# Hybrid decoder trunk with a product-key expert FFN: expert-slot transposes later among the hidden rows, the second half's first hidden rows in other PSUM banks, score products right behind the norms

## The chip, the cores and the metric

The kernel runs on one core of a Trainium2 chip. The metric is the device time of one execution in microseconds (us). The engines named below are PE (matrix products and transposes, into PSUM), DVE (vector work), ACT (activation functions and copies), POOL (elementwise work) and SP, which issues the transfers. Each engine works through its own list of instructions in the order in which the built program has them; an instruction that waits holds up everything behind it in that list.

## What is computed

Two layers; each adds an attention mixer and then an expert FFN to the residual `h`. The change lies in the expert FFN, which is in short:

```python
q = (xt @ wq).reshape(t, 8, 2, 128)
s = einsum('thpd,hpnd->thpn', q, sub_keys)        # scores: 8 heads x 2 halves x 64 keys per token
s_top, i_top = top_k(s, 16)
cand_s = s_top[:, :, 0, :, None] + s_top[:, :, 1, None, :]
best_s, best_j = top_k(cand_s, 16)                # 16 of 4096 experts per head and token
g = softmax(best_s)
h_all = xt @ u.T                                  # every token against all 4096 experts
a = gelu(h_all at the chosen experts) * g
out = (a scattered into t x 4096) @ v
```

## The kernel before

The 1040 tokens are four quarters. In each layer the FFN handles two halves of the tokens, P (quarters 0 and 1) and Q (quarters 2 and 3), one after the other; each half has two parts, called half 0 and half 1 in the code. The work of one such pair runs through these steps:

- `scores` (L987): PE products of the tokens with the keys; ACT copies the results out of PSUM (L992).
- `tops` (L996 to L1000): DVE takes the 16 best of 64 scores, five instructions for one group of 64 (`top16`). `combine` (L1018 to L1096) sums pairs, takes the best 16 of 64 candidates with `top16` again, makes the softmax (its result, `gS`, is written at L1045) and decodes the expert numbers into `mS` (L1092) and `rS` (L1094). All of it is DVE work but an exponential on ACT.
- `slots` (L1131, L1132, L1136): for each tile of 128 tokens PE transposes `mS`, `rS` and `gS` through PSUM banks 0 and 1 (ring `g`). DVE copies the first two out (L1133, L1134); ACT and DVE (L1139, L1140) read the third.
- `hidden` (L1113): for each of 32 rows of 128 experts PE forms `xt @ u.T` in 24 products of 512 columns (or 48 of 272 and 256), from weights that are split into a high and a low part. ACT applies gelu and writes row r of `G`.
- `gates` (DVE L1152 to L1157, PE L1164, DVE L1169): for 16 tokens at a time the choices are turned into a mask with 32 products and multiplied into `G`. In both calls that have gates they run among the later hidden rows, and need the slots.
- `values` (L1203): 32 rows of `G` times `v`, for 4 of the 8 output blocks (`d0`=0), then for the other 4 (`d0`=4). ACT and DVE split each row of `G` into high and low (L1196, L1197). At the end DVE adds the sums to `h` (L261, in `hupdate`), which frees the PSUM banks 4, 5, 6, 7, 2, 3 that held them.

While PE works on P's values, the choices for Q are prepared: `select` is a generator of norms (`apply`), then tops and combines of Q, and `values` takes steps of it after each row as long as a budget lasts (`bud`); what is left over is emitted by `run(todo)` before `hidden(l, Q, ...)`.

A scheduler then fixes the order on each engine, by a simulation of its own, under the dependences that the code order gives: an instruction that reuses a PSUM bank or a buffer stands behind the earlier users of it in the code. So the order on PE and DVE differs from the order in the code, and is read from the built program.

Of the kernel before, what the change touches and what calls it, by code (L numbers as in the profile page):

```python
# [22 lines left out]
LAG = 1  # L23
HQ = 8
PR = 13
START = 0
MM = ((3, 0, 2, 0, 0, 3, 0, 0), (3, 0, 2, 0, 0, 3, 0, 0))
PEND = 31
# [31 lines left out]
def tile_trunk(ctx, tc, h0, w_pk, wgate, w2, glab, w_out, wqT, keysT, u_pk, v_w, sinks,  # L60
# [100 lines left out]
    def set_rings(**kw):  # L161
        for tag, bs in kw.items():
            rings[tag] = [bs, 0]

    def ps1(tag="a"):
        r = rings[tag]
        r[1] += 1
        return banks[r[0][(r[1] - 1) % len(r[0])]]

    set_rings(d=(0, 1), o=(2,), a=(3, 4, 5, 6, 7), h=(6, 7, 2, 3), g=(0, 1), s=(4, 5), v=(4, 5, 6, 7, 2, 3))  # L170


    ident = const.tile([128, 128], F32, name="ident")
# [828 lines left out]
    def tops(P, half, cc):  # L1002

        nt = len(P.parts[half][1].tiles)
        V = sb([128, 3, 8, 16], F32, "V")
        I = sb([128, 3, 8, 16], U32, "I")
        P.V[half, cc] = V, I
        for a in range(8):
            for j in range(nt):
                top16(sv(P, half, 2 * cc + a // 4)[:, j, a % 4, :], V[:, j, a], I[:, j, a])  # L1010
                yield 1.3
# [84 lines left out]
    def cuts(P, halves):  # L1096

        if len(halves) == 2 and P.merge:
            return [(None, 0, P.sp.w)]
        return [(h, P.parts[h][0], P.parts[h][1].w) for h in halves]  # L1100

    def hidden(l, P, G, lo, hi, ring, cst=None, end=32):

        cs = cuts(P, (0, 1))
        for r in range(lo, hi):
            pss = [ps1(ring)[:, 0:w] for h, o, w in cs]
            for k in range(KT):
                if k % 4 == 0:
                    wh, wl = wpiece(u_pk[l, r][:, k * 128:(k + 4) * 128], f"u{l}_{r}_{k // 4}")
                ks = slice(k % 4 * 128, k % 4 * 128 + 128)  # L1110
                for i, (wt, low) in enumerate(((wh, 0), (wh, 1), (wl, 0))):
                    for ps, (h, o, w) in zip(pss, cs):
                        PE.matmul(ps, wt[:, ks], yv(h, low, k, 0, w // 2 if h is None else w),  # L1113
                                  start=(k == 0 and i == 0), stop=(k == KT - 1 and i == 2))
            for ps, (h, o, w) in zip(pss, cs):
                n = min(max(sum(P.gated) - o, 0), w)
                if n:
                    ga = sb([128, 512], F32, "ht")
                    ACT.activation(ga[:, 0:n], ps[:, 0:n], AF.Gelu)
                    POOL.tensor_tensor(G[:, r, o:o + n], ga[:, 0:n], G[:, r, o:o + n], op=ALU.mult)  # L1120
                if n < w:
                    ACT.activation(G[:, r, o + n:o + w], ps[:, n:w], AF.Gelu)
            P.rows = r + 1
            while cst and sum(P.gated) < P.sp.w and sum(P.gated) * (end - lo) < P.sp.w * (r + 1 - lo):
                gates(P, int(P.gated[0] == P.parts[0][1].w), G, *cst)

    def slots(P, half):

        for j, (o, m) in enumerate(P.parts[half][1].tiles):
            tp = ps1("g").bitcast(F16)[:, 0:256].rearrange("p (a b) -> p a b", a=2)  # L1130
            PE.transpose(tp[:, 0, 0:m], P.mS[0:m, j, :], ident16[0:m, 0:m])  # L1131
            PE.transpose(tp[:, 1, 0:m], P.rS[0:m, j, :], ident16[0:m, 0:m])  # L1132
            DVE.tensor_copy(P.mT[half][:, o:o + m], tp[:, 0, 0:m])  # L1133
            DVE.tensor_copy(P.rT[half][:, o:o + m], tp[:, 1, 0:m])  # L1134
            tg = ps1("g")
            PE.transpose(tg[:, 0:m], P.gS[0:m, j, :], ident[0:m, 0:m])  # L1136
            g4 = tg[:, 0:m].rearrange("p (b t) -> p b t", t=4)
            gh, gl = [P.gg[half][:, o // 4:(o + m) // 4, a] for a in range(2)]
            ACT.activation(gh, g4, AF.Copy, scale=GSC)  # L1139
            DVE.scalar_tensor_tensor(gl, g4, GSC, gh, op0=ALU.mult, op1=ALU.subtract)  # L1140
# [33 lines left out]
    def values(l, P, G, halves, d0, todo=iter(()), work=(), bud=0.0, hs=None, reuse=True):  # L1174


        cs = cuts(P, halves)
        work = dict(work)
        accs = [[None] * len(cs) for d in range(4)]
        for i, (h, o, w) in enumerate(cs):  # L1180
            for d in range(4):
                if w <= 256 and d % 2:
                    accs[d][i] = (bank[:, 256:256 + w], False, True)
                else:
                    bank = ps1("v")
                    accs[d][i] = (bank[:, 0:w], True, w > 256)
        done = []
        left = 0.0
        for r in range(32):
            wh, wl = wpiece(v_w[l][:, r, d0 * 128:d0 * 128 + 512], f"v{l}_{r}_{d0}" if reuse else None)  # L1190
            parts = []
            for h, o, w in cs:
                tg = "2" if w > 272 else ""
                ah = sb([128, w], F32R, "ah" + tg)
                al = sb([128, w], F32R, "al" + tg)
                ACT.activation(ah, G[:, r, o:o + w], AF.Copy)  # L1196
                last = DVE.tensor_tensor(al, G[:, r, o:o + w], ah.bitcast(F32), op=ALU.subtract)  # L1197
                parts.append((ah, al))
            done.append(last.ins)
            for d in range(4):  # L1200
                for i, (wt, low) in enumerate(((wh, 0), (wh, 1), (wl, 0))):
                    for (ps, opens, closes), pr in zip(accs[d], parts):
                        PE.matmul(ps, wt[:, d * 128:d * 128 + 128], pr[low], start=(opens and r == 0 and i == 0),  # L1203
                                  stop=(closes and r == 31 and i == 2))
            if r in work:
                work.pop(r)()
            if len(done) > LAG:
                left += bud
                with tc.issue_after(done[-1 - LAG]):
                    while left > 0:  # L1210
                        left -= next(todo, 99)
        for d in range(4):
            for (ps, _, _), (h, o, w) in zip(accs[d], cs):
                for half in (0, 1) if h is None else (h,):
                    sp = P.parts[half][1]
                    p = ps[:, half * sp.w:half * sp.w + sp.w] if h is None else ps
                    if hs is not None and half == 1:
                        DVE.tensor_tensor(hs[:, d0 + d], hs[:, d0 + d], p, op=ALU.add)
                        continue
                    ht = hload(2 * l + 1, d0 + d, sp)  # L1220
                    hupdate(2 * l + 2, d0 + d, sp, ht, p)
        return todo

    def run(*gens):
        for _ in itertools.chain(*gens):
            pass
# [40 lines left out]
    for l in range(DEPTH):  # L1267
# [49 lines left out]
            run(combine(P, 0, 0, *tabs), combine(P, 0, 1, *tabs))  # L1317
        for c in range(4):
            scores(l, P, c, (1,), "s")
        slots(P, 0)  # L1320
        run(tops(P, 1, 0), combine(P, 1, 0, *tabs))
        hidden(l, P, G, 0, 4, "h")
        run(tops(P, 1, 1), combine(P, 1, 1, *tabs))
        slots(P, 1)
        rb = rstd(2 * l + 1, qs[2])
        rb2 = rstd(2 * l + 1, qs[3])
        hidden(l, P, G, 4, PR, "h")
        hidden(l, P, G, PR, 32, "h", cst, PEND)
        Q = peer_setup(qs[2], qs[3], False)
        scored = []  # L1330

        def select():

            for q, x, r in ((qs[2], Y[0], rb), (qs[3], Y[1], rb2)):
                for k in range(KT):
                    apply(2 * l + 1, q, gf, x, r, (k,), buf="xb")
                    yield 1.0
            for half in range(2):
                for cc in range(2):
                    for gen in (tops(Q, half, cc), combine(Q, half, cc, *tabs) if half == 0 else iter(())):  # L1340
                        while len(scored) < 2 * cc + 2:
                            yield 99
                        yield from gen
                if half == 0:
                    slots(Q, 0)

        work = {5 * c + 9: lambda c=c: scored.append(scores(l, Q, c, (0, 1), "g")) for c in range(4)}
        todo = values(l, P, G, (0, 1), 0, select(), work, 2.4)
        todo = values(l, P, G, (0, 1), 4, todo, (), 1.8)
        run(todo)  # L1350
        hidden(l, Q, G, 0, HQ, "h")
        run(combine(Q, 1, 0, *tabs), combine(Q, 1, 1, *tabs))
        slots(Q, 1)
        hidden(l, Q, G, HQ, 32, "h", cst, QE)
        more = l + 1 < DEPTH
        if more:
            rb = rstd(2 * l + 2, quarters[0])
# [86 lines left out]
```

## Time and profile before

| | |
|---|---|
| median of three runs | 3353.25 us (3343.89 to 3354.38) |
| the profiled execution | 3348.59 us, span of its instructions 3346.8 us |
| PE busy | 3139.3 us, 94% of the span |
| DVE busy | 2074.0 us, 62% |
| ACT, POOL busy | 1311.1 us (39%), 958.4 us (29%) |
| granted PE clock, mean | 0.959 |

The span runs from the first to the last instruction; 1.8 us of the execution lie around it. Busy shares are means over the whole program: the FFN has stretches in which DVE works without a pause while PE waits for it.

### The profile page before, as it was taken

To read this page: it belongs to the slowest core of one execution; us is meant where nothing else is said; L and a number is where in the kernel's file an instruction comes from. 1 tells how busy PE (TensorE), PEld (TensorE's weight loads), DVE (VectorE), ACT (ScalarE), POOL (GpSimd) and SP (SyncE) were. 2 spreads that over 40 slices of the span, in tenths; PEclk is the share of its full clock that TensorE was granted. 3 is DMA by queue.
4 is the path that set the end of the run, shared out by engine and by line. 5 is a ranking of instruction groups with operands and counts; after the bars stand their busy time and mean duration, and the time that the engine had idled before them with its cause. 6 is when DMAs were issued, how large, how long until landed. Compare 5 with 4: busy or idle time off the path is not lost.

```text
span 3346.8 us, 65733 instructions
## 1 busy us (share of the span) xinstructions
PE 3139.3 (94%) x23453; PEld 2636.6 (79%) x23453; DVE 2074.0 (62%) x6694; ACT 1311.1 (39%) x3013; POOL 958.4 (29%) x976
## 2 busy tenths in 40 slices
PE   7999999988999988999898999999889999899998
PEld 7686887768999987888874878877668888688788
DVE  4546446689885389753225464457796835986457
ACT  4534334424334343324344343344333344343354
POOL 4314021313454341010401131213244524301135
PEclk9899998989999999999997999999799999999999
DMA  8767774736346555446964677757454466554665
GB/s 292 235 194 251 248 258 136 215 127 236 128 137 191 182 174 172 157 145 200 333 232 141 211 263 241 251 161 238 149 181 148 154 191 219 172 179 143 195 191 169
DMA packets 406442, 655.56 MB, mean 196 GB/s; under 512 B 44560, under 2 KB 122464, under 8 KB 406112
## 3 DMA queue, kind: packets, MB, share of 16 engines
q1 hardware_dynamic: 406112, 651.35, 60.3%
q8 instruction: 184, 3.01, 0.4%
q14 instruction: 146, 1.20, 0.1%
HBM read 492.70 MB, written 158.47 MB: 195 GB/s over the span
## 4 chain that ended last, share of the span: by engine, by line
PE 67%; DVE 20%; DMA 7%; ACT 2%; issue 2%; SPq 1%; POOL 1%; DVEq 0%; POOLq 0%; ACTq 0%
PE b L1113 18%; PE b L1203 15%; PE b L335 13%; PE b L1164 4%; PE b L987 3%; PE b L703 2%; DVE arena_r L1197 2%; DMA arena<-h 2%; DVE arena L998 2%; DVE arena L1000 2%; DVE arena L997 2%; PE b L618 2%; PE b L757 2%; DMA arena<-in_w_pk_dram 1%; DVE arena L999 1%
## 5 line engine op out<-in xcount | busy, mean ns | idle before, releaser
L281 POOL TENSOR_TENSOR arena_r<-arena,arena_r 128x512 fp32r<-128x512 f32 (+1 forms) x440 | 555.4, 1268 | 869.5 <-ACT arena_r L274 800.3
L1113 PE MATMUL b<-arena_r 128*128 128x512 f32 (+2 forms) x3840 | 763.0, 357 | 17.5 <-DVE arena L261 15.5
L1203 PE MATMUL b<-arena_r 128*128 128x512 f32 (+2 forms) x4224 | 749.7, 337 | 31.4 <-DVE arena_r L1197 24.6
L1203 PEld LDWEIGHTS b<-arena_r 128*128 128x128 f32 x4224 | 643.8, 190 | 126.2 <-DVE arena_r L1197 35.7
L335 PE MATMUL b<-arena_r 128*128 128x256 f32 (+1 forms) x4992 | 702.6, 295 | 36.4 <-ACT arena_r L274 10.0
L1113 PEld LDWEIGHTS b<-arena_r 128*128 128x128 f32 x3840 | 626.0, 191 | 115.6 <-DVE arena L261 16.2
L335 PEld LDWEIGHTS b<-arena_r 128*128 128x128 f32 x4992 | 643.9, 196 | 76.3 <-issue 19.7
L274 ACT ACTIVATE arena_r<-arena 128x512 fp32r<-128x512 f32 x456 | 285.1, 629 | 479.8 <-PE b L1113 104.1
L1197 DVE TENSOR_TENSOR arena_r<-arena,arena_r 128x512 fp32r<-128x512 f32 (+2 forms) x352 | 270.8, 783 | 314.6 <-ACT arena_r L1196 313.5
L308 ACT ACTIVATE arena_r<-arena 128x512 fp32r<-128x512 f32 x288 | 181.2, 631 | 384.3 <-PE b L1203 120.9
L987 PE MATMUL b<-arena_r 128*128 128x256 f32 (+1 forms) x1632 | 208.9, 283 | 3.4 <-DMA arena_r<-m_3l 1.8
L987 PEld LDWEIGHTS b<-arena_r 128*128 128x128 f32 (+1 forms) x1632 | 196.5, 183 | 13.5 <-issue 4.4
L1152 DVE TENSOR_TENSOR arena<-arena 128x2048 f16<-128x2048 f16 x129 | 176.1, 1367 | 45.3 <-PE b L1164 45.3
L257 POOL TENSOR_TENSOR arena<-arena 128x256 f32<-128x256 f32 (+1 forms) x126 | 107.9, 856 | 315.1 <-ACT arena L256 312.4
L1120 POOL TENSOR_TENSOR arena<-arena 128x32 f32<-128x32 f32 (+25 forms) x91 | 98.5, 1089 | 305.4 <-ACT arena L1171 206.6
L1196 ACT ACTIVATE arena_r<-arena 128x512 fp32r<-128x512 f32 (+2 forms) x352 | 172.2, 502 | 31.1 <-PE b L1203 27.6
L1164 PEld LDWEIGHTS <-arena 128*128 128x128 f16 x4128 | 144.4, 118 | 17.2 <-issue 14.4
L1169 DVE SCALAR_TENSOR_TENSOR arena<-b,arena 128x224 f32<-128x224 f32 (+20 forms) x129 | 63.1, 499 | 145.9 <-PE b L1164 145.7
L1164 PE MATMUL b<-arena 128*128 128x32 f16 x4128 | 152.3, 190 | 0.0
L715 DVE TENSOR_TENSOR_SCAN arena<-arena,zf 128x384 f32<-128x384 f32 (+6 forms) x116 | 104.1, 900 | 76.5 <-ACT arena L710 75.5
L421 ACT ACTIVATE arena<-b 128x256 f32<-128x256 f32 (+1 forms) x144 | 55.2, 384 | 211.7 <-PE b L335 211.2
L1157 DVE TENSOR_TENSOR arena<-arena 128x1024 f16<-128x1024 f16 x129 | 123.3, 956 | 0.1
(267 smaller groups left out, 3796.7 us busy)
## 6 DMA issues: line engine op xcount, KB each, us to landing
arena<-in_v_w_dram SPq DMA_DIRECT2D x288, 256.0 KB, 2.9
arena<-in_u_pk_dram SPq DMA_DIRECT2D x256, 256.0 KB, 3.0
arena_r<-a_0h SPq DMA_DIRECT2D x108, 256.0 KB, 3.7
arena_r<-a_0l SPq DMA_DIRECT2D x108, 256.0 KB, 3.9
arena_r<-a_1h SPq DMA_DIRECT2D x108, 256.0 KB, 3.2
arena_r<-a_1l SPq DMA_DIRECT2D x108, 256.0 KB, 3.5
arena<-m SPq DMA_DIRECT2D x96, 256.0 KB, 4.5
arena<-h SPq DMA_DIRECT2D x192, 128.0 KB, 3.1
```

Source lines behind the costliest of these rows:

```text
L274: ACT.activation(hi, src, AF.Copy)
L281: e.tensor_tensor(lo[:, a:b], src[:, a:b], hi[:, a:b].bitcast(F32), op=ALU.subtract)
L308: ACT.activation(hi, wload(src), AF.Copy)
L335: PE.matmul(ps, wt[:, ks], x.at(low, k, xo, sp.w), start=(k == 0 and i == 0), stop=(k == KT - 1 and i == 2))
L987: PE.matmul(ps, yv(half, low, k, o, m), wt[:, kk * 256:kk * 256 + 256], start=(k == 0 and i == 0 and e == 0), stop=(k == KT - 1 and i == 2 ...
L1113: PE.matmul(ps, wt[:, ks], yv(h, low, k, 0, w // 2 if h is None else w), start=(k == 0 and i == 0), stop=(k == KT - 1 and i == 2))
L1152: DVE.tensor_tensor(Lh, iotaM.unsqueeze(1).to_broadcast([128, 4, 128, 4]), v4(P.mT[half], 128), op=ALU.is_equal)
L1157: DVE.tensor_tensor(R, R0.unsqueeze(2).to_broadcast([128, 4, 2, 32, 4]), P.gg[half][:, t0 // 4:t0 // 4 + 4].unsqueeze(3).to_broadcast([128 ...
L1164: PE.matmul(ps[:, i * 32:(i + 1) * 32], Lh[:, b, :, t], R[:, b, part, :, t], start=(part == 0), stop=(part == 1))
L1196: ACT.activation(ah, G[:, r, o:o + w], AF.Copy)
L1197: last = DVE.tensor_tensor(al, G[:, r, o:o + w], ah.bitcast(F32), op=ALU.subtract)
L1203: PE.matmul(ps, wt[:, d * 128:d * 128 + 128], pr[low], start=(opens and r == 0 and i == 0), stop=(closes and r == 31 and i == 2))
```

## The change

Three things are moved. In the first half, the transposes of P's half 0 come after six hidden rows where they came before the first, with the combines of half 1 behind them, and those of half 1 stand at hidden row 19 (`PR + 6`), among the gates, where they came before row 4. In the second half, the first eight hidden rows use the PSUM banks 0, 1, 6, 7 (ring `hq`) where they used 6, 7, 2, 3, and the transposes of Q's half 1 stand at row 16 where they came before row 8. During P's values, the four score products of Q stand behind rows 8, 10, 12, 14 where they stood behind rows 9, 14, 19, 24; each then adds 9.0 to the budget, and the budgets per row are 2.1 and 1.6 where they were 2.4 and 1.8, with 0.8 charged for a norm where it was 1.0.

```diff
+HS = 8
...
-    set_rings(d=(0, 1), o=(2,), a=(3, 4, 5, 6, 7), h=(6, 7, 2, 3), g=(0, 1), s=(4, 5), v=(4, 5, 6, 7, 2, 3))
+    set_rings(d=(0, 1), o=(2,), a=(3, 4, 5, 6, 7), h=(6, 7, 2, 3), hq=(0, 1, 6, 7), g=(0, 1), s=(4, 5), v=(4, 5, 6, 7, 2, 3))
...
-    def hidden(l, P, G, lo, hi, ring, cst=None, end=32):
+    def hidden(l, P, G, lo, hi, ring, cst=None, end=32, jobs=()):
 
         cs = cuts(P, (0, 1))
+        jobs = dict(jobs)
         for r in range(lo, hi):
+            if r in jobs:
+                jobs[r]()
...
             if r in work:
-                work.pop(r)()
+                left += work.pop(r)() or 0.0
...
+        run(tops(P, 1, 0))
+        hidden(l, P, G, 0, 6, "h")
         slots(P, 0)
-        run(tops(P, 1, 0), combine(P, 1, 0, *tabs))
-        hidden(l, P, G, 0, 4, "h")
-        run(tops(P, 1, 1), combine(P, 1, 1, *tabs))
-        slots(P, 1)
+        run(combine(P, 1, 0, *tabs), tops(P, 1, 1), combine(P, 1, 1, *tabs))
         rb = rstd(2 * l + 1, qs[2])
         rb2 = rstd(2 * l + 1, qs[3])
-        hidden(l, P, G, 4, PR, "h")
-        hidden(l, P, G, PR, 32, "h", cst, PEND)
+        hidden(l, P, G, 6, PR, "h")
+        hidden(l, P, G, PR, 32, "h", cst, PEND, {PR + 6: lambda: slots(P, 1)})
...
                     apply(2 * l + 1, q, gf, x, r, (k,), buf="xb")
-                    yield 1.0
+                    normed.append(k)
+                    yield 0.8
...
-        work = {5 * c + 9: lambda c=c: scored.append(scores(l, Q, c, (0, 1), "g")) for c in range(4)}
-        todo = values(l, P, G, (0, 1), 0, select(), work, 2.4)
-        todo = values(l, P, G, (0, 1), 4, todo, (), 1.8)
+        def score(c):
+            assert len(normed) == 2 * KT
+            scores(l, Q, c, (0, 1), "g")
+            scored.append(c)
+            return 9.0
+
+        work = {2 * c + HS: lambda c=c: score(c) for c in range(4)}
+        todo = values(l, P, G, (0, 1), 0, select(), work, 2.1)
+        todo = values(l, P, G, (0, 1), 4, todo, (), 1.6)
         run(todo)
-        hidden(l, Q, G, 0, HQ, "h")
+        hidden(l, Q, G, 0, HQ, "hq")
         run(combine(Q, 1, 0, *tabs), combine(Q, 1, 1, *tabs))
-        slots(Q, 1)
-        hidden(l, Q, G, HQ, 32, "h", cst, QE)
+        hidden(l, Q, G, HQ, 32, "h", cst, QE, {HQ + 8: lambda: slots(Q, 1)})
```

In the changed file the lines stand a few numbers lower: the hidden products L1113 are L1117 there, the transposes L1131, L1132 and L1136 are L1135, L1136 and L1140, the value products L1203 are L1207. (So an L1136 means `gS` in a row of before, and `rS` in a row of the changed program.)

What the scheduler makes of it is shown at two places. The first is PE's list where Q's hidden rows begin, in layer 0 (layer 1 has the same pattern). Names are the PSUM bank written (`b0_65` is bank 0) and the buffers read; `x12` is twelve such instructions in a row. Before:

```order
L1203 MATMUL b3_68<-arena_r_63 128x256 x5
L1113 MATMUL b2_67<-arena_r_63 128x512 x12
L1113 MATMUL b6_71<-arena_r_63 128x512 x24
L1113 MATMUL b7_72<-arena_r_63 128x512 x22
L1136 MATMUL b0_65<-ident_73,arena_64 128x128
L1113 MATMUL b7_72<-arena_r_63 128x512 x2
L1113 MATMUL b2_67<-arena_r_63 128x512 x12
L1113 MATMUL b3_68<-arena_r_63 128x512 x14
L1136 MATMUL b0_65<-ident_73,arena_64 128x128
L1113 MATMUL b3_68<-arena_r_63 128x512 x10
L1113 MATMUL b6_71<-arena_r_63 128x512 x24
L1113 MATMUL b7_72<-arena_r_63 128x512 x24
```

Behind these 144 products come the transposes L1131 of `mS` and L1132 of `rS`, apart from each other, with 8 and 27 products between them. After:

```order
L1207 MATMUL b3_68<-arena_r_63 128x256 x5
L1117 MATMUL b6_71<-arena_r_63 128x512 x12
L1140 MATMUL b0_65<-ident_73,arena_64 128x128 x2
L1117 MATMUL b0_65<-arena_r_63 128x512 x24
L1117 MATMUL b6_71<-arena_r_63 128x512 x12
L1117 MATMUL b7_72<-arena_r_63 128x512 x12
L1135 LDWEIGHTS arena_64
L1135 MATMUL b1_66<-ident16_78,arena_64 128x128
L1136 LDWEIGHTS arena_64
L1136 MATMUL b1_66<-ident16_78,arena_64 128x128
```

Both transposes of `gS` moved from behind 58 and 86 products to behind 12, and those of `mS` and `rS` from behind 144 to behind 60. Hidden row 0 now writes bank 0 and row 1 bank 1, which the transposes of `slots(Q, 0)`, earlier in the code, use too, so both stand behind them. After the rows shown a second L1135 and L1136 follow at once, then 24 products in bank 1; the first gate products (L1168) stand behind 216 hidden products, where they stood behind 277.

The second place is PE's list in the first half of layer 1, from the end of hidden row 4 on. Before:

```order
L1113 MATMUL b7_72<-arena_r_63 128x512 x2
L1131 LDWEIGHTS arena_64
L1131 MATMUL b1_66<-ident16_78,arena_64 128x128
L1113 MATMUL b7_72<-arena_r_63 128x512 x9
L1132 LDWEIGHTS arena_64
L1132 MATMUL b1_66<-ident16_78,arena_64 128x128
L1113 MATMUL b7_72<-arena_r_63 128x512 x13
L1113 MATMUL b2_67<-arena_r_63 128x512 x9
```

After:

```order
L1117 MATMUL b7_72<-arena_r_63 128x512 x24
L1135 LDWEIGHTS arena_64
L1135 MATMUL b1_66<-ident16_78,arena_64 128x128
L1136 LDWEIGHTS arena_64
L1136 MATMUL b1_66<-ident16_78,arena_64 128x128
L353 MATMUL b0_65<-ones_82,arena_64 128x1
L1117 MATMUL b2_67<-arena_r_63 128x512 x24
L1117 MATMUL b3_68<-arena_r_63 128x512 x5
```

The first transpose of `mS` moved from behind 122 hidden products to behind 144, that of `rS` from behind 131 to behind 144 as well. The six transposes of half 1, which before stood behind 218 to 288 products, stand behind 484 and 505 now, past the first gates.

## Rows read from the trace of the kernel before

**Rows 1.** Waits of PE over the whole span: us in total, times, longest.

```profile
PE b L1203 <- DVE arena_r L1197: 24.6, 27, 2.7
PE b L1131 <- DVE arena L1092: 17.2, 4, 7.5
PE b L1113 <- DVE arena L261: 15.5, 2, 9.6
...
PE b L1136 <- DVE arena L1045: 7.5, 3, 5.1
...
PE b L1136 <- DVE arena L1140: 4.1, 4, 1.6
```

**Rows 2.** Stretches: start:end, length, busy by engine (instructions), granted PE clock, DMA.

```profile
780.00:840.00 60.00, 47.99 (x388) 47.11 (x388) 60.00 (x331) 20.47 (x40) 29.41 (x20) 0.96 0.55 178
...
1176.00:1287.00 111.00, 101.34 (x760) 98.60 (x760) 101.03 (x501) 44.23 (x99) 39.58 (x32) 0.94 0.54 171
...
1296.20:1300.30 4.10, 4.06 (x11) 3.23 (x12) 4.10 (x33) 1.46 (x4) 1.57 (x3) 0.62 0.41 132
1300.30:1331.00 30.70, 30.70 (x135) 24.85 (x134) 30.70 (x187) 14.62 (x24) 2.88 (x3) 1.00 0.61 193
...
2923.00:2957.00 34.00, 34.00 (x140) 27.26 (x140) 34.00 (x211) 16.64 (x28) 3.60 (x4) 0.93 0.57 183
```

**Rows 3.** PE in order of time, layer 0, first half: start, length, [idle before].

```profile
839.69 0.19 PE L1131 MATMUL b<-ident,arena 16*128 16x16 f16 x1 [7.54 <-DVE arena L1092]
839.81 3.66 PE L1113 MATMUL b<-arena_r 128*128 128x256 f32 x15
```

**Rows 4.** PE in order of time, layer 1, first half.

```profile
2472.26 0.29 PE L1131 MATMUL b<-ident,arena 128*128 128x128 f16 x1 [6.35 <-DVE arena L1092]
2472.30 4.19 PE L1113 MATMUL b<-arena_r 128*128 128x512 f32 x9
...
2502.99 0.48 PE L1136 MATMUL b<-ident,arena 128*128 128x128 f32 x1 [5.14 <-DVE arena L1045]
...
2536.68 2.31 PE L1164 MATMUL b<-arena 128*128 128x32 f16 x64
```

**Rows 5.** DVE in order of time, layer 1, first half.

```profile
2482.20 0.21 DVE L1134 COPY arena<-b 128x128 f16<-128x128 f16 x1
...
2513.24 3.46 DVE L1152 TENSOR_TENSOR arena<-arena 128x2048 f16<-128x2048 f16 x2
...
2518.97 0.69 DVE L1157 TENSOR_TENSOR arena<-arena 128x1024 f16<-128x1024 f16 x1
```

**Rows 6.** PE in order of time, layer 0, where Q's hidden rows begin.

```profile
1283.83 2.75 PE L1203 MATMUL b<-arena_r 128*128 128x272 f32 x21
1296.24 15.13 PE L1113 MATMUL b<-arena_r 128*128 128x512 f32 x58 [9.65 <-DVE arena L261]
...
1317.83 13.68 PE L1113 MATMUL b<-arena_r 128*128 128x512 f32 x58
1331.35 0.23 PE L1131 MATMUL b<-ident,arena 128*128 128x128 f16 x1
```

**Rows 7.** DVE in order of time, in the same stretch.

```profile
1284.32 0.43 DVE L1197 TENSOR_TENSOR arena_r<-arena,arena_r 128x256 fp32r<-128x256 f32 x1
...
1308.31 0.28 DVE L1045 TENSOR_TENSOR arena<-arena 128x128 f32<-128x128 f32 x1
...
1329.53 0.43 DVE L1092 COPY arena<-arena 128x128 f16<-128x128 f16 x1
...
1331.43 0.43 DVE L1094 COPY arena<-arena 128x128 f16<-128x128 f16 x1
```

**Rows 8.** Layer 1, where Q's hidden rows begin: PE, then DVE.

```profile
2922.66 15.00 PE L1113 MATMUL b<-arena_r 128*128 128x512 f32 x54 [5.89 <-DVE arena L261]
...
2957.70 0.23 PE L1131 MATMUL b<-ident,arena 128*128 128x128 f16 x1
...
2954.51 0.43 DVE L1092 COPY arena<-arena 128x128 f16<-128x128 f16 x1
```

More of the change, by code (lines that the diff above doesn't have):

```diff
@@ L1319, in tile_trunk @@
             scores(l, P, c, (1,), "s")
+        run(tops(P, 1, 0))
+        hidden(l, P, G, 0, 6, "h")
         slots(P, 0)
-        run(tops(P, 1, 0), combine(P, 1, 0, *tabs))
-        hidden(l, P, G, 0, 4, "h")
-        run(tops(P, 1, 1), combine(P, 1, 1, *tabs))
-        slots(P, 1)
+        run(combine(P, 1, 0, *tabs), tops(P, 1, 1), combine(P, 1, 1, *tabs))
         rb = rstd(2 * l + 1, qs[2])
         rb2 = rstd(2 * l + 1, qs[3])
-        hidden(l, P, G, 4, PR, "h")
-        hidden(l, P, G, PR, 32, "h", cst, PEND)
+        hidden(l, P, G, 6, PR, "h")
+        hidden(l, P, G, PR, 32, "h", cst, PEND, {PR + 6: lambda: slots(P, 1)})
         Q = peer_setup(qs[2], qs[3], False)
-        scored = []
+        scored, normed = [], []
         def select():
```

## The prediction, on record before the changed kernel ran

> **What bounds the kernel now.** The page's busy times come first: PE works 94% of the span, DVE 62%. So the end is set by PE's own work and by the moments at which it waits. The waits of PE, summed by what they waited for, show where [rows 1]. Two kinds belong to this change: transposes of `slots` that wait for the choices on DVE (17.2 + 7.5 + 4.1 = 28.8 us in 11 waits) and the first hidden rows of the second half, which wait until DVE has emptied a PSUM bank of `values` (15.5 us in two waits, one per layer). Together 44.3 us, 1.3% of the span; that is the most that moving instructions past these waits could give, the half clock behind them aside. A third kind, 24.6 us in 27 waits, is `values` waiting for DVE's low parts.
>
> Then the stretches [rows 2]. While PE stands at slots or at a bank, DVE is not late by chance: it is busy 60.00 of 60.00 us in 780 to 840, 30.70 of 30.70 in 1300.3 to 1331, 34.00 of 34.00 in 2923 to 2957. In these stretches DVE sets the time at which choices are ready, and PE's list only decides how much other work PE has done by then. That is the question to ask of each move: **how many hidden products stand ahead of a transpose, and when does DVE deliver what it reads?** A transpose that moves back in the list lets PE do more first; one that moves forward makes PE wait longer, however few the other waits become.
>
> The prices: a hidden product of 512 columns takes 13.68/58 = 0.236 us at full clock [rows 6]; one DVE instruction in the busy stretches takes 101.03/501 = 0.20 us on average [rows 2].
>
> **First half, layer 0.** Before, PE stands 7.54 us at 839.69, at the first transpose of `mS`, with 367 hidden products done [rows 3]. DVE has no gap from 780 on, and up to the L1092 that ends this wait its order is the same in both programs but for one 0.3 us instruction. So this time stays. In the new order 360 products and two transposes of `gS` stand ahead of that point; the waits ahead of it grow together instead of going away (the second transpose of `gS` waits for DVE's copy of the first, which now stands close to that same L1092). No gain to here. Behind it the transposes of half 1 are gone from the path to the gates: [rows 1] less the three long waits of [rows 3, 4] (7.54, 6.35, 5.14) leave 9.8 us in eight short ones, of which I put 4 us here. The half clock behind 839.81 is paid in both. With about 2 us for fewer broken stretches and 1 to 2 us lost again at the transposes that now stand among the gates I take **-4 us**. Bounds: -8 (nothing lost there) and +1 (the one long wait costs more clock).
>
> **First half, layer 1.** Here the gain is real. At 2472.26 a wait of 6.35 us ends, behind 122 products, and the next nine products take 4.19 us where 2.1 would do [rows 4]. In the new order 144 products stand ahead, and `rS` follows at once; it is written some 3.5 us behind `mS`, so at about 2476.3 PE has done 144 where it had done 131: 3 us won. From there to the first gate products at 2536.68 before takes 60.4 us for 205 products, 48.4 us of work; the rest is the wait of 5.14 us at 2502.99, smaller ones and half clock. After, 192 products (45.3 us) and one wait: the second tile's transposes need bank 1, which DVE's copies free; these stand 38 instructions behind L1092 before, ending at 2482.4 [rows 5], and 57 behind it now, so about 4.5 us later, near 2487, while PE arrives near 2483. Gates could begin at 2476.3 + 45.3 + 4.5 = 2526. DVE has the first masks (L1152) done at 2516.7 and starts on what multiplies them at 2519.0 [rows 5], so it is ready. That is 10.5 us won; less 1.5 for the transposes among the gates, **-9 us**. Bounds -14 (no wait at the copies) and -4 (DVE as late as PE).
>
> **Second half, layer 0.** The bank wait before is 9.65 us, then 58 products take 15.13 us, 1.4 more than at full clock [rows 6]. Banks 0 and 1 are not held by `values`, but `slots(Q, 0)` uses them, and it stands ahead of the hidden rows in the code; so hidden row 0 is behind the transposes of `gS`, and row 1 behind those of `mS` and `rS`. In the new order PE has only 12 products, in bank 6, ahead of the first, and 60 ahead of the other pair. When does DVE deliver? Before, from its last L1197 at 1284.32 to L1045 at 1308.31, L1092 at 1329.53 and L1094 at 1331.43 [rows 7]; between the first and L1092 stand 218 instructions, and 233 in the new order: 15 x 0.20 = 3 us more. Ahead of that, between the same two L1197 that bound the second part of `values`, 321 stand where 353 stood: 32 x 0.20 = 6.4 us less, since 13 groups of `top16` now run ahead of it where 9 did. So 3.4 us earlier by work, and up to 10 us more if the gaps in 1176 to 1287 (111.00 - 101.03) all closed [rows 2]. I take 5 us: L1092 near 1325. L1094 and DVE's copies between the two pairs add some 4 us, so at 1329 PE has 60 products done. Before it has 144 at 1331.35, thus 134 at 1329. **74 products behind, 74 x 0.236 = +17.5 us.** Behind this point both lists hold the same work for PE, and before has no wait there to win back. Bounds: all gaps closed, L1092 at 1316, gives 60 products at 1320.5, where before has 98: +9. No gain from `values` and the 15 instructions in full: 60 at 1337 against 168: +25.5.
>
> The scores move ahead without a price on PE: the same products stand in another place, and before their results were used it was DVE that idled. The budgets give little: while the scores are missing the generator answers 99, so `left` falls near -97, and even four times 9.0 doesn't bring it above zero before this call of `values` ends, in either version. The 13 groups come from the part that `run(todo)` emits and the scheduler hoists.
>
> **Second half, layer 1.** The same order, and nearly the same trace: a bank wait of 5.89 us, DVE without a gap, L1092 at 2954.51 and 152 products done at 2957.70 [rows 8]. With 5 us as above PE has 60 at 2954 against 136: **+18 us**, bounds as above.
>
> **The clock.** Behind the bank wait the granted clock is 0.62 for 4.1 us, a mixture of the two levels of 1.2 and 2.4 GHz, and 1.00 after that [rows 2]: one wait of 9.65 us costs about 1.5 us more. The new order has several waits in a row in each second half; I add 1 us a layer, since most of the slow work falls into time in which PE would wait anyway. The Trainium skill ("TensorE: Matmul & The Clock Gate", "What's actually happening") puts it the other way about: throttled is the default, and activity releases it. By that rule each wait of the row could start again at the low level, and as an estimate from it the sum would be some 4 us higher; no row here shows several waits that close together.
>
> **Sum.** -4 - 9 + 17.5 + 18 + 2 = +24.5 us on the profiled execution's 3348.6 (1.8 us of it around the span): **3373 us**. That execution lies 4.7 us under the median of the three runs, 3353.25, and inside their spread of 10.5 us; 0.3% is 10 us, about what a measurement of this kernel can tell from no change.
>
> **Rivals.** *The waits really go (faster).* Were `gS` and `mS` of the second half ready when PE comes to them, the bank waits (9.65 + 5.89 and some 3 of half clock) would vanish on top of the first halves' 13: about 3317 to 3330. It decides at L1045 and L1092: they would have to come some 18 us earlier, near 1290 and 1311. For it speaks that DVE idles in the first part of `values`, so that work could go there; against it that only four more groups do, in the new order. Chance 0.10. *It evens out.* `values` loses its waits on DVE, all gaps close, and the second halves cost +9 each against -13 or -18: 3346 to 3358. For it speak the 24.6 us of waits in [rows 1]. Chance 0.17. *Worse.* No gain in `values`, each wait with its own slow stretch: +25 a layer, little won in the first halves: 3392 to 3405. Chance 0.10. *As forecast,* 3358 to 3392: 0.63.
>
> The range leaves out the tail on each side: 3348 to 3392. Slower by over 0.3% takes in the forecast and the worse case: 0.73; within 0.3% 0.17; faster 0.10.
>
> **What would show it.** In the changed profile: at the start of Q's hidden rows PE runs 12 products, stands for over 10 us in all at bank 6 and the transposes of `gS` (released by DVE), then runs 48 and stands again at `mS`; 60 products done when L1092's successor ends, near 40 us behind the last low part. In layer 1's first half one short wait instead of 6.35 and 5.14. PE's waits on slots grow from 28.8 us to about 60, those on banks shrink little. I am wrong if DVE reaches `gS` of Q's half 0 within some 10 us of its last low part, if the hidden rows don't wait for the slots in banks 0 and 1, or if `values` gets shorter by over 10 us a layer.

## The result, and the profile after

The changed kernel takes **3382.72 us** (median of four executions, 3380.71 to 3386.49), against 3349.61 for the kernel before (median of four): ratio 1.0101, 95% interval 1.008 to 1.0122. It is slower by 33 us, where +24.5 (3373 us) was forecast. Its profiled execution has a span of 3380.9 us, 34.1 us more than before.

The waits of PE over the whole span, in the columns of [rows 1] (the program's lines stand 1 to 4 further down: L1113 is now L1117, L1131 L1135, L1136 L1140, L261 L262, L1045 L1046, L1092 L1093, L1203 L1207):

```profile
PE b L1207 <- DVE arena_r L1201: 21.7, 24, 3.3
PE b L1117 <- DVE arena L262: 21.2, 2, 10.6
PE b L1140 <- DVE arena L1144: 17.6, 4, 10.9
PE b L1140 <- DVE arena L1046: 13.5, 2, 6.9
...
PE b L1135 <- DVE arena L1093: 8.8, 3, 3.5
...
PE b L1117 <- DVE arena L1144: 4.7, 2, 2.5
...
PE b L1136 <- DVE arena L1062: 3.5, 1, 3.5
```

The bank waits grew from 15.5 to 21.2 us. With some small ones (3.3 and 2.0 us) the waits of transposes come to 48.7 us where they were 28.8, and hidden rows wait another 4.7 and 1.5 us for DVE's copies out of the slots' banks: 55 us, where the forecast said about 60.

Where Q's hidden rows begin in layer 0, PE and then DVE, which answers to [rows 6, 7]:

```profile
1287.73 5.38 PE L1117 MATMUL b<-arena_r 128*128 128x512 f32 x12 [10.57 <-DVE arena L262]
1299.99 0.47 PE L1140 MATMUL b<-ident,arena 128*128 128x128 f32 x1 [6.88 <-DVE arena L1046]
1303.71 0.48 PE L1140 MATMUL b<-ident,arena 128*128 128x128 f32 x1 [3.24 <-DVE arena L1144]
1306.37 10.69 PE L1117 MATMUL b<-arena_r 128*128 128x512 f32 x38 [2.19 <-DVE arena L1144]
1317.67 2.58 PE L1117 MATMUL b<-arena_r 128*128 128x512 f32 x10 [0.61 <-DMA arena_r<-u_0l]
1322.61 0.23 PE L1135 MATMUL b<-ident,arena 128*128 128x128 f16 x1 [2.36 <-DVE arena L1093]
1324.48 0.29 PE L1136 MATMUL b<-ident,arena 128*128 128x128 f16 x1 [1.65 <-DVE arena L1040]
...
1326.36 33.93 PE L1117 MATMUL b<-arena_r 128*128 128x512 f32 x137 [0.77 <-DVE arena L1138]
```
```profile
1273.50 0.76 DVE L1201 TENSOR_TENSOR arena_r<-arena,arena_r 128x272 fp32r<-128x272 f32 x2
...
1299.65 0.28 DVE L1046 TENSOR_TENSOR arena<-arena 128x128 f32<-128x128 f32 x1
...
1322.13 0.42 DVE L1093 COPY arena<-arena 128x128 f16<-128x128 f16 x1
```

The reader should count: 12 products, a stand at both transposes of `gS`, 38 + 10 more, a stand at `mS`. At 1326.36 PE has 60 products done; before, it had 144 at 1331.35 [rows 6]. DVE delivers `mS` 7.4 us earlier than before, which is far less than the 84 missing products (84 x 0.236 = 19.8 us). Layer 1 does the same, later (PE, then DVE; it answers to [rows 8]):

```profile
2929.05 5.46 PE L1117 MATMUL b<-arena_r 128*128 128x512 f32 x12 [10.61 <-DVE arena L262]
2941.16 0.48 PE L1140 MATMUL b<-ident,arena 128*128 128x128 f32 x1 [6.66 <-DVE arena L1046]
...
2965.19 0.23 PE L1135 MATMUL b<-ident,arena 128*128 128x128 f16 x1 [3.53 <-DVE arena L1093]
...
2968.95 6.41 PE L1117 MATMUL b<-arena_r 128*128 128x512 f32 x20 [0.77 <-DVE arena L1138]
```
```profile
2915.08 0.67 DVE L1201 TENSOR_TENSOR arena_r<-arena,arena_r 128x512 fp32r<-128x512 f32 x1
...
2964.71 0.42 DVE L1093 COPY arena<-arena 128x128 f16<-128x128 f16 x1
```

To set the stretches beside the forecast, PE's order in time gives marks that every version has: the first hidden product of a layer (before: 780.40 and 2436.14), the first product of the second part of P's `values` (1173.01, 2811.65), the start of Q's last hidden product (1513.52, 3137.95) and of the last value product of all (3333.39). The change of each stretch's length against before, in us:

| stretch | forecast | changed kernel |
|---|---|---|
| all ahead of the first hidden row | 0 | +2.5 |
| layer 0, first half and first part of values | -4 | -7.0 |
| layer 0, second part of values and Q's hidden rows | +17.5 +1 | +20.5 |
| Q's values and the attention of layer 1 | 0 | -4.9 |
| layer 1, first half and first part of values | -9 | -2.5 |
| layer 1, second part of values and Q's hidden rows | +18 +1 | +25.3 |
| the rest | 0 | +0.4 |
| sum | +24.5 | +34.3 |

Each stretch is read from one profiled execution of a version. Executions of one kernel lie some 10 us apart (3342.55 to 3353.33 us in 15 of the kernel before), so two or three us in one row show nothing by themselves.

### The profile page after: what moved, and what is told of

It is laid out like the page before. It is cut to its first block, busy times and chain, and to the rows that moved or that the text cites. A ratio compares the mean times of both kernels' runs of the same rounds, so it can differ in the third digit from the quotient of the medians.

```text
span 3380.9 us, 65755 instructions
## 1 busy us (share of the span) xinstructions
PE 3150.3 (93%) x23453; PEld 2641.8 (78%) x23453; DVE 2099.7 (62%) x6694; ACT 1314.5 (39%) x3013; POOL 957.0 (28%) x976
## 4 chain that ended last, share of the span: by engine, by line
PE 67%; DVE 20%; DMA 6%; ACT 2%; issue 2%; POOL 1%; SPq 1%; DVEq 0%; POOLq 0%; ACTq 0%
PE b L1117 18%; PE b L336 14%; PE b L1207 14%; PE b L1168 4%; PE b L988 3%; PE b L704 2%; DMA arena<-h 2%; DVE arena L1001 2%; DVE arena L999 2%; DVE arena L998 2%; DVE arena_r L1201 2%; PE b L619 2%; PE b L758 1%; DVE arena L1000 1%; DVE arena L997 1%
## 5 line engine op out<-in xcount | busy, mean ns | idle before, releaser
L1117 PE MATMUL b<-arena_r 128*128 128x512 f32 (+2 forms) x3840 | 766.7, 358 | 28.3 <-DVE arena L262 21.2
L1207 PE MATMUL b<-arena_r 128*128 128x512 f32 (+2 forms) x4224 | 743.7, 336 | 29.4 <-DVE arena_r L1201 21.7
L1207 PEld LDWEIGHTS b<-arena_r 128*128 128x128 f32 x4224 | 643.8, 190 | 121.9 <-DVE arena_r L1201 30.9
L1117 PEld LDWEIGHTS b<-arena_r 128*128 128x128 f32 x3840 | 629.6, 192 | 129.8 <-issue 21.8
L1201 DVE TENSOR_TENSOR arena_r<-arena,arena_r 128x512 fp32r<-128x512 f32 (+2 forms) x352 | 283.8, 821 | 288.4 <-ACT arena_r L1200 287.3
L1200 ACT ACTIVATE arena_r<-arena 128x512 fp32r<-128x512 f32 (+2 forms) x352 | 172.2, 502 | 26.5 <-PE b L1207 20.5
L1168 PEld LDWEIGHTS <-arena 128*128 128x128 f16 x4128 | 144.1, 118 | 17.9 <-issue 14.8
L1168 PE MATMUL b<-arena 128*128 128x32 f16 x4128 | 151.9, 190 | 0.6 <-DVE arena L1161 0.6
L1173 DVE SCALAR_TENSOR_TENSOR arena<-b,arena 128x224 f32<-128x224 f32 (+22 forms) x129 | 62.5, 499 | 104.6 <-PE b L1168 104.6
```

Source lines behind the costliest of these rows:

```text
L1168: PE.matmul(ps[:, i * 32:(i + 1) * 32], Lh[:, b, :, t], R[:, b, part, :, t], start=(part == 0), stop=(part == 1))
```

## The experiments

The theory: the second halves lose because the free banks tie hidden rows 0 and 1 behind the transposes of Q's first choices, so that PE comes to them with 12 and 60 products done; the first halves gain; the scores' place is worth little. The rivals: the scores and budgets are what costs; the banks cost by themselves; or the moved transposes gain nothing. All runs were timed in five rounds beside the kernel before, which stood at 3346.75 us for the first four and 3348.68 us for the other four.

**The old banks.** The changed kernel with

```diff
-        hidden(l, Q, G, 0, HQ, "hq")
+        hidden(l, Q, G, 0, HQ, "h")
```

> The changed kernel with one edit: the first eight hidden rows of the second half are back on the ring of banks 6, 7, 2, 3. Theory (the free banks are what costs, since their rows are tied behind the transposes of slots(Q, 0)): 65 hidden products stand ahead of the first transpose of gS and 156 ahead of the first mS, where the changed kernel has 12 and 60, so the second halves lose nothing against the kernel before; the first halves' 8 us and the shorter values' 5 to 7 us stay: 3330 to 3340 us. Rival (the scores' new place and the budgets cost the time, and the banks only show it): 3365 to 3385 us. Rival (both share it): 3345 to 3360 us.

Measured: **3312.69 us**, ratio 0.9898 (0.9881 to 0.9916). One letter turns a loss of 1% into a gain of 1%. The rivals about the scores are out. The theory has the sign and the place, but the time is 17 us under its lower end; most of that lies between the layers, where nothing is edited (last section).

**The banks alone.** The kernel before with

```diff
+hq=(0, 1, 6, 7)
-        hidden(l, Q, G, 0, HQ, "h")
+        hidden(l, Q, G, 0, HQ, "hq")
```

> The kernel before with one edit: the first eight hidden rows of the second half on banks 0, 1, 6, 7. Theory: the order of the products is that of the changed kernel (12 ahead of gS, 60 ahead of mS), but DVE starts on the choices no earlier than before, so each layer loses some 24 us and nothing is won elsewhere: 3385 to 3405 us, slower than the changed kernel. Rival (the free banks are harmless or a gain by themselves, the scores and budgets cost): 3330 to 3355 us.

Measured: **3376.27 us**, ratio 1.0093 (1.0077 to 1.0108). The bank edit alone brings nearly the whole loss. Its second halves are 21.8 and 26.8 us longer, 48.6 in all, as forecast; 17.3 us come back between the layers, which the expectation did not have, so the time is 9 us under its lower end, and below the changed kernel's, where slower was expected. Its first halves, in which nothing is edited, are 2.3 and 2.5 us shorter than before.

**The first half alone.** The kernel before with the edits to P:

```diff
+        run(tops(P, 1, 0))
+        hidden(l, P, G, 0, 6, "h")
         slots(P, 0)
-        run(tops(P, 1, 0), combine(P, 1, 0, *tabs))
-        hidden(l, P, G, 0, 4, "h")
...
+        hidden(l, P, G, PR, 32, "h", cst, PEND, {PR + 6: lambda: slots(P, 1)})
```

> The kernel before with the first half's edits alone (order of tops, slots and combine, transposes of half 1 at row 19); scores, budgets, banks and the second half's slots as before. Theory: the trace of the changed kernel has the first half of layer 0 some 6 us shorter and that of layer 1 3 to 6 us: 3338 to 3344 us. Rival (the moved transposes only shift waits to the gates): 3347 to 3353 us.

Measured: **3333.11 us**, ratio 0.9959 (0.9945 to 0.9972). Both first halves are shorter, by 5.6 and 5.2 us, against 2.3 and 2.5 without the edit in the banks alone; 4.3 us lie between the layers. The time is 5 us under the theory's lower end. The rival is out.

**Late slots.** The changed kernel, with the transposes of Q's half 0 behind the first use of banks 0 and 1:

```diff
-                if half == 0:
-                    slots(Q, 0)
...
-        hidden(l, Q, G, 0, HQ, "hq")
+        hidden(l, Q, G, 0, HQ, "hq", jobs={6: lambda: slots(Q, 0)})
```

> The changed kernel with one edit: the transposes of the second half's first choices leave the generator and stand as a job in front of hidden row 6, behind the rows that use banks 0 and 1 for the first time. So the banks stay free, but 144 products stand ahead of gS and 191 ahead of mS. Theory: no bank wait at the start of Q's hidden rows and hardly a wait at the transposes, as DVE has the choices some 40 us behind its last low part and PE needs 34 us for 144 products: against the kernel before both bank waits (9.65 and 5.89 us, with some 3 us of half clock) and the first halves' 8 us are won, and 5 us of values: 3310 to 3328 us. Rival (DVE sets the end of the stretch, as it must wait for the later transposes before it writes the next choices into the same tiles, and the gates start later): 3330 to 3350 us.

Measured: **3302.42 us**, ratio 0.9862 (0.9846 to 0.9877), the fastest of all, 1.4% below the kernel before and 2.4% below the changed one. It is 7.6 us under the theory's lower end; 10.4 us lie between the layers. PE where Q's hidden rows begin in layer 0:

```profile
1274.30 10.13 PE L1117 MATMUL b<-arena_r 128*128 128x512 f32 x43
1285.96 22.51 PE L1117 MATMUL b<-arena_r 128*128 128x512 f32 x96 [1.53 <-DVE arena L262]
1308.31 0.27 PE L1140 MATMUL b<-ident,arena 128*128 128x128 f32 x1
...
1319.45 0.23 PE L1135 MATMUL b<-ident,arena 128*128 128x128 f16 x1
...
1328.28 0.23 PE L1135 MATMUL b<-ident,arena 128*128 128x128 f16 x1
```

The bank wait has shrunk to 1.53 us (0.67 in layer 1), and no transpose has a wait in its brackets. The same four banks that cost 49 us with the transposes ahead of them now save most of the bank wait. The Trainium skill ("Perfetto Trace Analysis", "Matmuls") says that independent matmul groups should rotate through different PSUM banks, so that one group's evacuation lies beside the next one's products. The run of the banks alone shows where the stress lies: rows behind a transpose that waits for DVE are not independent, and there the same rotation lost 48.6 us.

**Late slots at row 4**, a smaller dose: `jobs={4: ...}` where the kernel above has 6.

> The kernel with the late transposes (in front of hidden row 6), now in front of row 4: 96 products ahead of the first gS and 156 ahead of the first mS in layer 0 (178 in layer 1), instead of 144 and 191. A dose of the theory that PE loses what it lacks in products when DVE delivers mS: there DVE writes mS at 1317.5 and 2916.4 and PE would come to it at about 1311.5 and 2917, so it waits some 6 us in layer 0 and hardly in layer 1: 3304 to 3314 us, against 3302.4 at row 6. Rival (the place of the transposes matters only through the banks): 3300 to 3304 us.

Measured: **3322.96 us**, ratio 0.9929 (0.9915 to 0.9942). The direction is right, the size and the place are not. PE in layer 0:

```profile
1303.66 0.27 PE L1140 MATMUL b<-ident,arena 128*128 128x128 f32 x1
1304.32 0.73 PE L1117 MATMUL b<-arena_r 128*128 128x512 f32 x2 [0.38 <-ACT arena_r L309]
1307.58 2.57 PE L1117 MATMUL b<-arena_r 128*128 128x512 f32 x10 [2.53 <-DMA arena_r<-u_0l]
1309.98 0.27 PE L1140 MATMUL b<-ident,arena 128*128 128x128 f32 x1
1313.83 14.04 PE L1117 MATMUL b<-arena_r 128*128 128x512 f32 x48 [3.58 <-DVE arena L1144]
1327.71 0.23 PE L1135 MATMUL b<-ident,arena 128*128 128x128 f16 x1
```

There is no wait at `mS`, where I expected 6 us. PE stands earlier: 2.53 us for weights (`u_0l`) and 3.58 us for DVE's copy of `gS` (L1144), which frees the bank of the next hidden row. The second halves are 11.3 and 6.9 us longer than with row 6 (these two stands make 6.1 of the 11.3), and 6.9 of the 20 us lie ahead of the first hidden row, which no edit touches. So this run doesn't show that a missing product costs its duration; the stands of PE are for other things.

**The ring turned.** The changed kernel with the same four banks in another order:

```diff
-hq=(0, 1, 6, 7)
+hq=(6, 7, 0, 1)
```

> The changed kernel with the same four banks in another order, 6, 7, 0, 1: so 48 products stand ahead of the first gS and 108 ahead of the first mS, instead of 12 and 60. Theory: 48 products more at 0.236 us are 11.3 us a layer when PE waits for mS, 22.6 us in all: 3352 to 3368 us, still slower than before. Rival (what costs is that banks 0 and 1 stand in the ring at all, or the scores): 3375 to 3390 us. Rival (the bank wait at the start takes all of it): 3380 us.

Measured: **3348.71 us**, ratio 1.0002 (0.9993 to 1.0011); 34 us faster than the changed kernel, and 3 us under the theory's lower end. PE where Q's transposes of `mS` stand in layer 0:

```profile
1324.28 0.23 PE L1135 MATMUL b<-ident,arena 128*128 128x128 f16 x1 [1.97 <-DVE arena L1093]
...
1327.97 7.37 PE L1117 MATMUL b<-arena_r 128*128 128x512 f32 x20 [0.77 <-DVE arena L1138]
```

The second halves are 13.5 and 12.0 us longer than before, the changed kernel's 20.5 and 25.3: the 48 products bring 7.0 + 13.3 = 20.3 us, where 22.6 were worked out. Most of the rest is again between the layers (-16.3 against -4.9). So the rival that the banks cost by standing in the ring is out: what 48 more products ahead of the transposes bring back is close to their duration. The 25.5 us that stay against before fit the same reading: PE has 108 products done at 1327.97, 161.2 us into this stretch, where before had about 156; 48 products are 11.3 us of the 13.5 in layer 0.

**Late slots with the old scores.** Late slots at row 6, with

```diff
-        work = {2 * c + HS: lambda c=c: score(c) for c in range(4)}
-        todo = values(l, P, G, (0, 1), 0, select(), work, 2.1)
-        todo = values(l, P, G, (0, 1), 4, todo, (), 1.6)
+        work = {5 * c + 9: lambda c=c: score(c) for c in range(4)}
+        todo = values(l, P, G, (0, 1), 0, select(), work, 2.4)
+        todo = values(l, P, G, (0, 1), 4, todo, (), 1.8)
```

and 1.0 charged for a norm, 0.0 added for a score.

> The kernel with the late transposes (row 6), with the scores back at rows 9, 14, 19, 24 of values and the old budgets (2.4, 1.8, and 1.0 for a part of the norms). Theory: the scores' place and the budgets are worth 3 to 6 us, through a few groups of top16 earlier in values, as the kernel with the first half alone has the first values 2 us and the one with old banks 4 us shorter than before: 3302 to 3312 us. Rival (scores and budgets carry the gain that is left between the first half alone, 3333, and the changed kernel on its old banks, 3313): 3318 to 3325 us.

Measured: **3310.31 us**, ratio 0.9885 (0.987 to 0.99). Scores and budgets are worth about 8 us there, where 3 to 6 were expected (a loose size: the intervals of the two ratios, 0.987 to 0.99 and 0.9846 to 0.9877, overlap a little); 5.6 us of them lie in layer 0's second part of values and Q's hidden rows (-8.5 against -14.1).

**Late slots with the old banks.** Late slots at row 6, and

```diff
-        hidden(l, Q, G, 0, HQ, "hq", jobs={6: lambda: slots(Q, 0)})
+        hidden(l, Q, G, 0, HQ, "h", jobs={6: lambda: slots(Q, 0)})
```

> The kernel with the late transposes (row 6), its first eight hidden rows back on banks 6, 7, 2, 3. Theory: with the old banks the transposes stood behind enough products anyway (65 and 156, no wait at them), so moving them further back gives nothing, and the bank waits of 8.3 and 2.6 us stay: as the changed kernel on its old banks, 3308 to 3318 us. Rival (the late transposes are a gain by themselves, the banks do nothing): 3300 to 3305 us.

Measured: **3310.75 us**, ratio 0.9894 (0.9879 to 0.9909), as the changed kernel on its old banks (3312.69). Moving the transposes gains nothing by itself; it is what makes the free banks usable.

The stretches of all runs, in us against before, with the products that the program's order has ahead of the first `gS` and the first `mS` of Q in layer 0 (before: 58 and 144):

| run | products | first half, layers 0 and 1 | second half, layers 0 and 1 | between |
|---|---|---|---|---|
| changed kernel | 12, 60 | -7.0, -2.5 | +20.5, +25.3 | -4.9 |
| banks alone | 12, 60 | -2.3, -2.5 | +21.8, +26.8 | -17.3 |
| ring turned | 48, 108 | -6.8, -2.5 | +13.5, +12.0 | -16.3 |
| late slots, row 4 | 96, 156 | -6.3, -4.4 | -2.8, +0.8 | -11.8 |
| old banks | 65, 156 | -7.3, -4.8 | -5.5, -2.6 | -15.2 |
| late slots, old banks | 144, 151 | -7.3, -7.7 | -6.0, -2.9 | -16.6 |
| late slots, old scores | 144, 183 | -6.3, -3.3 | -8.5, -5.5 | -8.4 |
| late slots | 144, 191 | -6.1, -4.2 | -14.1, -6.1 | -10.4 |
| first half alone | 58, 144 | -5.6, -5.2 | -1.7, -0.2 | -4.3 |

In the first three rows the second halves follow the products: the fewer, the longer. Where the products are as many as before or more, they no longer decide: row 4 of the late slots, with 96 and 156, is longer than the old banks with 65 and 156; its PE row above shows stands for weights and for the bank of `gS`.

## Why the prediction was right, and where its sizes were off

**The mechanism of the second halves** held in each step: 12 products, a stand at the bank and at `gS`, 48 more, a stand at `mS`, with the old banks and the turned ring as the test. 60 products were forecast for 1329 and were done at 1326.36, though 4.5 us of that are only an earlier start. The sign "near 40 us behind the last low part" did not fit the text's own sum (45.2 + 3 to `mS`): it was 48.3 us to `mS` and 52.6 to the products behind it. "Those on banks shrink little" was wrong in sign: they grew by 5.7 us, 0.9 in layer 0 and 4.7 in layer 1. In layer 1, before, twelve products in bank 2 and two short stands filled part of the time in which the next bank was awaited; ten of these products are the row

```profile
2914.16 2.60 PE L1113 MATMUL b<-arena_r 128*128 128x512 f32 x10 [1.39 <-DMA arena_r<-u_0l]
```

In the changed order nothing stands ahead of the wait for bank 6.

**Second half, layer 0** (+18.5 forecast with the clock, +20.5 measured). The 5 us by which `mS` was to come earlier were -7.4 us on the clock (1322.13 against 1329.53), of which -4.5 is only that this stretch begins earlier; 2.9 are left, 2 us fewer than taken. The parts: from the last low part to `mS` before 45.2 us [rows 7], now 48.3 by the DVE rows above from the second of the two low parts (at about 1273.8): the 3 us for 15 instructions were right. The 6.4 us that `values` gives were met as well (101.33 to 94.90 us in the windows below), but by luck of the price: 0.20 us is for a record of the trace, and the 32 are instructions of the program, which has fewer of them (the trace has 46 records fewer, 494 to 448). By its own count the price was 101.33/353 = 0.29 us, and 32 would have been 9.2 us; the ones that left are shorter than the mean.

**Second half, layer 1** (+19 forecast, +25.3 measured) is the larger mis-sized term. I carried the 5 us over from layer 0 and did not look at layer 1's own `values`. There `mS` comes at 2964.71, 10.2 us later than before, and the stretch begins 8.5 us later: 1.7 us late where 5 early were taken. That is 6.7 us, which covers the miss of 6.3. The windows of the second part of `values` show where it lies, layer 0 and then layer 1, before and after:

```profile
1173.00:1284.30 111.30, 100.68 (x753) 97.56 (x752) 101.33 (x494) 45.87 (x104) 41.57 (x34) 0.94 0.54 172
...
2811.70:2908.40 96.70, 88.36 (x373) 68.84 (x372) 92.77 (x460) 40.03 (x72) 44.87 (x34) 1.00 0.62 201
```
```profile
1168.50:1273.80 105.30, 97.68 (x744) 96.23 (x743) 94.90 (x448) 45.12 (x103) 41.60 (x34) 0.94 0.57 180
...
2820.20:2915.10 94.90, 87.83 (x372) 68.77 (x371) 90.15 (x418) 39.91 (x72) 45.03 (x34) 1.00 0.64 203
```

DVE's busy time (the third column with a count) falls by 6.4 us in layer 0, but by 2.6 us in layer 1, which is 1.8 us shorter in all; from there to `mS` DVE takes 3.5 us more (46.1 and 49.6 us). One low part more (1.3 us) stands in that window after; why else it falls by less stays open. Its gaps stay (10.0 and 10.4 us in layer 0, 3.9 and 4.8 in layer 1), so the rival in which they close did not come.

**First half, layer 0** (-4 forecast, -7.0 measured): the waits did grow together, into one of 10.86 us at 835.15, at the second transpose of `gS`, behind DVE's copy of the first (L1144), as the text said:

```profile
835.15 0.48 PE L1140 MATMUL b<-ident,arena 128*128 128x128 f32 x1 [10.86 <-DVE arena L1144]
```

The gain behind them was 3 us larger than taken.

**First half, layer 1** (-9 forecast, -2.5 measured) was over-sized; -2.5 is also what the banks alone show without an edit there. The sign of one short wait in place of 6.35 and 5.14 us did not come: PE has four, 2.90, 3.45, 0.83 and 2.51 us.

```profile
2485.28 0.23 PE L1135 MATMUL b<-ident,arena 128*128 128x128 f16 x1 [2.90 <-DVE arena L1093]
2488.96 0.29 PE L1136 MATMUL b<-ident,arena 128*128 128x128 f16 x1 [3.45 <-DVE arena L1062]
...
2489.43 9.20 PE L1117 MATMUL b<-arena_r 128*128 128x512 f32 x29
2499.46 0.22 PE L1135 MATMUL b<-ident,arena 128*128 128x128 f16 x1 [0.83 <-DVE arena L1138]
...
2507.39 0.71 PE L362 MATMUL b<-ident,arena 128*128 128x128 f32 x4 [2.51 <-DVE arena L1138]
2507.86 6.67 PE L1117 MATMUL b<-arena_r 128*128 128x512 f32 x21
...
2542.64 2.31 PE L1168 MATMUL b<-arena 128*128 128x32 f16 x64
...
2678.95 1.24 PE L1168 MATMUL b<-arena 128*128 128x32 f16 x32 [0.56 <-DVE arena L1161]
2681.76 4.42 PE L1207 MATMUL b<-arena_r 128*128 128x512 f32 x11 [1.57 <-ACT arena_r L1200]
```

This layer's first hidden row starts at 2447.20, 11.1 us later than before. From there the gates begin after 95.4 us, where they began after 100.5 [rows 4]: 5.1 us won, not 10.5. Of the missing 5.4, PE loses 1.6 by `rS`, which it passes that much later than forecast: DVE's `mS` (L1093, 2485.22) ends 38.0 us behind the first hidden row, 2.0 later than before. Behind it one wait of 4.5 us was allowed for; in its place stand waits of 0.83 and 2.51 us (the second at a norm's broadcast, L362, for a bank that DVE's copies free), and slow products behind each stand: 29 take 9.20 us, 2.4 more than at 0.236 each, and 21 take 6.67, 1.7 more, at a granted clock of 0.73 and 0.74. The step had priced the waits and left out the clock behind them. Another 3.5 us go where `values` begins: the last gate comes right ahead of it, and PE waits for the ACT split of `G`'s first row; before, 15 products lay between.

**The clock** (+2). The granted clock is 0.70 from 1276.9 to 1326.4 and 0.60 in the 5.0 us behind:

```profile
1276.90:1326.40 49.50, 20.78 (x70) 14.71 (x68) 49.36 (x333) 12.56 (x22) 5.95 (x8) 0.70 0.30 95
1326.40:1331.40 5.00, 5.00 (x14) 3.94 (x15) 4.86 (x31) 0.34 (x1) 0.00 (x0) 0.60 0.00 0
```

0.4 x 5.0 = 2.0 us, against 1.5 before (0.62 for 4.1 us [rows 2]): half a microsecond in layer 0, not 1. In layer 1 it is 1.7 us (0.67 for 5.1 us) against 2.4 before (0.93 for 34.0 us [rows 2]), so nothing. Each wait does bring the slow products back: 12 take 5.38 us, 0.45 each, and the next 38 take 10.69 us, 1.7 more than at 0.236. That agrees with the rule of the Trainium skill ("TensorE: Matmul & The Clock Gate", "What's actually happening") that throttled is the default. But those products lie ahead of the next wait, which DVE ends, so only the last stretch costs time, and the 4 us that the rule would have added did not come here.

**Left out** were the stretch between the layers (-4.9) and the 2.5 us by which the first hidden row starts later. That the sum came within 10 us is in part luck: layer 1 took 6.5 us more than forecast in its first half and 6.3 in its second, and -4.9 between the layers and -3.0 in the first half of layer 0, for which the text had no reason, took back 7.9.

## What to carry to other kernels

A free PSUM bank is free only if its last user in program order comes early: before a group of products is put on another bank, look which instruction used that bank last, and when the engine delivers what that one waits for. Where another engine is saturated and sets the time of a result, count the independent products that stand ahead of the instruction that reads it; each one missing cost about its own duration here (48 products, 20.3 us where 22.6 were worked out), and waits that merely move say nothing. Two edits can each be worthless or harmful and pay together, as the free banks (+1%) and the late transposes (no gain) did: with both the kernel takes 3302.42 us, with neither (the old banks) 3312.69.

## What was not expected

The stretch from Q's hidden rows of layer 0 to the first hidden row of layer 1, above all the attention of layer 1, which no edit touches, is 4 to 17 us shorter in every version. Windows from Q's last product of values in layer 0 to the first hidden row of layer 1, then a stretch near its end, for the kernel before and then for the banks alone:

```profile
1775.60:2436.10 660.50, 611.25 (x4528) 481.03 (x4527) 392.95 (x1305) 265.99 (x671) 145.79 (x178) 0.93 0.65 209
2375.60:2425.60 50.00, 41.14 (x294) 39.25 (x295) 40.02 (x221) 13.47 (x30) 8.95 (x8) 0.84 0.71 232
```
```profile
1796.30:2439.00 642.70, 598.27 (x4528) 472.31 (x4527) 387.75 (x1305) 267.82 (x672) 145.85 (x178) 0.96 0.65 214
2396.30:2439.00 42.70, 39.66 (x320) 38.18 (x320) 42.56 (x257) 17.93 (x36) 8.87 (x8) 1.00 0.96 333
```

The same 4528 products take 13.0 us less PE time at a granted clock of 0.96 instead of 0.93; at the end it is 1.00 where it was 0.84. The order on PE differs there, since the scheduler places this stretch anew with each edit before it: of the 4526 products and transposes that start in it before, compared in the order of the traces by line, names and shape, 599 stand elsewhere in the banks alone (-17.3 us), 423 to 575 in the six other versions with -8.4 to -16.6, but 125 in the changed kernel (-4.9) and 169 in the first half alone (-4.3). That the order is what raises the clock was not tried apart, and which of the moved rows does it stays open. For a reader the size counts: 10 us and more between two versions of this kernel can come from a place that no edit names, so the gain of an edit is read from its own stretch.
